# A two-layer streaming encoder on one core: weight units of the seven-product down projections made in five steps, and where those steps stand

## The chip, the cores and the metric

The kernel runs on one NeuronCore of a Trainium2 chip. The metric is device time in microseconds (us) of one execution; lower is better. Five engines work beside each other, each through its own queue in order: TensorE (PE, matmuls, with its weight loads shown apart as PEld), VectorE (DVE), ScalarE (ACT), GpSimd (POOL) and SyncE (SP, which here only issues DMA transfers). They meet through semaphores.

## The reference

One inference step of a two-layer hybrid encoder, for 512 prompt tokens and 32 sample tokens, which the kernel carries side by side as 544 columns. Each layer is a token mixer (an S5 state-space layer in layer 0, multi-scale retention in layer 1), memory cross-attention, and a causal ConvFFN, each with a residual. The change lies in the ConvFFN:

```python
def conv_ffn(h, conv_state, w_up, conv_w, conv_b, w_down):
    l = h.shape[1]
    u = h.astype(F32) @ w_up.astype(F32)
    a, g = jnp.split(u, 2, axis=-1)
    ext = jnp.concatenate([conv_state.astype(F32), a], axis=1)
    cw = conv_w.astype(F32)
    conv = cw[0] * ext[:, 0:l] + cw[1] * ext[:, 1:l + 1] + cw[2] * ext[:, 2:l + 2] + conv_b.astype(F32)
    y = (jax.nn.gelu(conv) * g) @ w_down.astype(F32)
    return y.astype(h.dtype), ext[:, l:]
```

Here `w_up` is 1024 x 5632 and `w_down` 2816 x 1024, all in float32.

## The kernel before

**Arithmetic.** Tokens lie along the free dimension, in two halves of 272 columns (`TH`). A float32 product is made of three matmuls on split operands: each operand is a rounded high part and a low part (the difference), and high x high, high x low and low x high are accumulated. `split` (L227) makes the two parts: a copy on ACT (L228), a subtraction on DVE (L229).

**Order.** The program is written with a tile framework (`TileContext(nc, schedule_with_timeline_sim=True)`, L1566): the text gives the operations and the buffers by tag and number, and a scheduler sets each engine's queue when the program is built. A buffer tag with `bufs=3` holds three tiles; a fourth waits until one is released.

**Up tiles.** `ffn_layer` (L1292) makes 22 feature tiles of 128 rows in three groups of 8, 8 and 6 (`FGROUPS`, L49). One pass of the loop (L1309) makes two dense tiles, one from `w_a` and one from `w_g` (`dense`, L272): each loads 512 KB of raw weights (tag `wr`, three buffers), splits them into `wh` and `wl` (three buffers each) and runs 8 x 6 = 48 matmuls. An epilogue on DVE, ACT and POOL (L1314 to L1328) makes the convolution, the gelu and the gate. After every second pass `tokens` (L1176) builds, out of two gated feature tiles, the seven right-hand operands of a 2 x 2 seven-product scheme, as high and low parts: b11, b21, b22 and the four sums t1 to t4.

**The down projection.** After each group `down` (L1196) multiplies the group's tiles with its part of `w_down`. Output tiles are taken in four pairs (`p` = 0 to 3); a pair takes seven products (`PRODUCTS`, L52) over `kps` = 4 or 3 pairs of input tiles, 3 x `kps` matmuls each, where the plain scheme would take eight. Each product is added into the residual `x` by DVE (`add`, L1226). A pair's products share two PSUM banks and a third for product 2 (`take`, L1241).

**Weight units.** The left-hand operands of a pair come as units (`unit_open`, L1139): a unit covers two input pairs (one for the odd rest; `unit_sizes`, L95), so that a pair has two units. A unit takes

- a load of the raw blocks into `wr` (SP, L1154),
- three sums into `ws`, one buffer: two on DVE (L1158, L1159), one on POOL (L1160),
- `hb`, the high part of the three plain blocks a11, a22, a12 (ACT, L1161), and `lb`, at first minus that (ACT, L1164); four buffers each,
- `wh`, the high part of the four sums (ACT, L1162), and `wl`, their low part (DVE, L1163); the same three buffers as the up tiles', except that every fourth unit (j % 4 == 1, L1146) has buffers of its own, `whx` and `wlx`,
- and `unit_close` (L1172): a transfer issued by POOL reads the plain blocks from memory again and adds them to `lb`, which makes it the low part.

Products 1, 2 and 4 use `hb` and `lb`, the others `wh` and `wl`.

**The order written out in `down`.** Pairs 0 and 1 are opened and closed first (L1249 to L1251), behind the last tokens in the text. Products 1 and 7 of both pairs and 2 of pair 0 are begun with all input pairs but the last (`early`) and finished with the last one (`late`), which needs the last tokens. For later pairs (L1266 on) a pair is closed just ahead of its product 1, and the next pair is opened as a whole behind product 3 of the pair before.

**Behind the layer.** `done` hands a finished output pair to `resid_done` (L320), which makes the next stage's operand parts `xh`, `xl` and the sum of squares. Retention's first two dense tiles go through `dense2` (L291): with `late=1` both tiles run over seven operands, with a hook that forms the norm's columns between them (`resid_r`, L378), and then over the last.

Of the kernel before, what the change touches and what calls it, by code (L numbers as in the profile page):

```python
# [9 lines left out]
F32 = mybir.dt.float32  # L10
F32R = mybir.dt.float32r
I32 = mybir.dt.int32
AF = mybir.ActivationFunctionType
# [4 lines left out]
P = 128  # L18
# [174 lines left out]
class Kernel:  # L193
# [942 lines left out]
            self.resid_done(m)  # L1136


    def unit_open(self, src, nk, j):  # L1139


        V, A, PL = self.nc.vector, self.nc.scalar, self.nc.gpsimd
        n = nk * P

        def buf(tag):
# [4 lines left out]
        raw = self.main.tile([P, 1024], F32, tag="wr", bufs=3, name=self.name("wr"))  # L1150
        hs, ls = buf("wh"), buf("wl")
        hb, lb = (self.fp.tile([P, 768], F32R, tag=t, bufs=4, name=self.name(t)) for t in ("hb", "lb"))
        sf = self.fp.tile([P, 1024], F32, tag="ws", bufs=1, name=self.name("ws"))[:, :4 * n]
        self.nc.sync.dma_start(out=raw[:, :4 * n], in_=src)  # L1154

        def two(a):
            return a.rearrange("p (b n) -> p b n", b=2)
        V.tensor_tensor(out=two(sf[:, :2 * n]), in0=two(raw[:, n:3 * n]), in1=raw[:, :n].unsqueeze(1).to_broadcast([P, 2, n]), op=OP.subtract)  # L1158
        V.tensor_tensor(out=sf[:, 2 * n:3 * n], in0=sf[:, n:2 * n], in1=raw[:, n:2 * n], op=OP.add)  # L1159
        PL.tensor_tensor(out=sf[:, 3 * n:], in0=raw[:, 3 * n:4 * n], in1=sf[:, 2 * n:3 * n], op=OP.subtract)  # L1160
        A.copy(hb[:, :3 * n], raw[:, n:4 * n])  # L1161
        A.copy(hs[:, :4 * n], sf)  # L1162
        V.tensor_tensor(out=ls[:, :4 * n], in0=sf, in1=hs[:, :4 * n].bitcast(F32), op=OP.subtract)  # L1163
        A.activation(out=lb[:, :3 * n], in_=hb[:, :3 * n].bitcast(F32), func=AF.Copy, scale=-1.0)  # L1164
        d = {}
        for q, name in enumerate(("a11", "a22", "a12")):
            d[name] = hb[:, q * n:(q + 1) * n], lb[:, q * n:(q + 1) * n]
        for q, name in enumerate(("s3", "s1", "s2", "s4")):
            d[name] = hs[:, q * n:(q + 1) * n], ls[:, q * n:(q + 1) * n]
        return d, lb[:, :3 * n], src[:, n:4 * n]  # L1170

    def unit_close(self, u):  # L1172

        self.nc.gpsimd.dma_start(out=u[1], in_=u[2], accum_op=OP.add)

    def tokens(self, g):  # L1176

        V, A = self.nc.vector, self.nc.scalar
        t = [self.fp.tile([P, T + 4], F32, tag="f", bufs=FB, name=self.name("f"))[:, :T] for _ in range(2)]
# [6 lines left out]
        d = {}  # L1186
        for src, names in ((g[1], ("b21", "b22")), (t[0], ("t1", "t2")), (t[1], ("t3", "t4"))):
            hi, lo = self.parts(src)
            for h, name in enumerate(names):
                d[name] = hi[:, h * TH:(h + 1) * TH], lo[:, h * TH:(h + 1) * TH]  # L1190
        both = self.slot(dt=F32R)
        d["b11"] = both[:, :TH], both[:, TH:]
        self.split(b11, *d["b11"])
        return d

    def down(self, src, ys, done):  # L1196

        kps = len(ys)
# [3 lines left out]
        units = {}  # L1202

        def begin(p):
# [43 lines left out]
        early, late = range(kps - 1), [kps - 1]  # L1248
        for p in range(2):  # L1249
            begin(p)  # L1250
            end(p)  # L1251
        take(0)
        take(1)
        for i in (1, 7):
            step(0, i, early)
        for i in (1, 7):
            step(1, i, early)
        step(0, 2, early)
        for i in (1, 7, 2):
            step(0, i, late)  # L1260
        step(0, 6)
        step(0, 4)
        for i in (1, 7):
            step(1, i, late)
        step(0, 5)
        for p in range(1, KT // 2):  # L1266
            if p > 1:
                end(p)
                take(p)
                step(p, 1)  # L1270
                step(p, 7)
            else:
                step(p, 2)
            step(p - 1, 3)
            done(2 * p - 2)
            done(2 * p - 1)
            if p + 1 < KT // 2 and p > 0:
                begin(p + 1)
            step(p, 6)
            if p > 1:  # L1280
                step(p, 2)
            step(p, 4)
            step(p, 5)
        step(KT // 2 - 1, 3)
        done(KT - 2)
        done(KT - 1)

    def ffn(self, l):
        with self.tc.tile_pool(name=f"ffn{l}", bufs=1) as self.fp:
# [2 lines left out]
    def ffn_layer(self, l):  # L1292
# [13 lines left out]
        self.resid_start(0 + 1 if l == 0 else None)  # L1306
        for n, size in enumerate(FGROUPS):
            ys, half = [], []
            for _ in range(size):  # L1309
                pa, pg = first if f == 0 else [self.dense(io[n_][l, f], xs) for n_ in ("w_a", "w_g")]  # L1310
                paf = pa.rearrange("p a b -> p (a b)")
                ext = slot(W + 2)

# [17 lines left out]
                    ys.append(self.tokens(half))  # L1331
                    half = []
                f += 1
            last = n == len(FGROUPS) - 1
# [256 lines left out]
```

## Time and profile before

| what | value |
|---|---|
| time, median of 3 runs | 1932.65 us (1930.83 to 1935.11) |
| profiled execution, its own time | 1933.26 us |
| its span in the trace | 1931.4 us |
| mean granted TensorE clock | 0.974 |
| matmuls of the down projections (L1224) | 1848 of 13551 |
| DMA, mean over the span | 105 GB/s |

The six down projections run from about 517 to 581, 668 to 730, 793 to 845, 1591 to 1655, 1742 to 1804 and 1867 to 1913 us. In a page of the profile, a group of instructions shows line, engine, operation, names of what it writes and reads, shape and count, then busy time and mean duration, then the engine's idle time just ahead of it and what ended that. A window row gives busy time and count of PE, PEld, DVE, ACT and POOL in a stretch, the granted clock, the busy share of the DMA engines and their rate.

### The profile page before, as it was taken

The page shows a single profiled execution, that of the slowest core. Times are in us where ns is not written, and L with a number is a line of the kernel's source. Part 1 is how long each engine was busy: PE and PEld are TensorE (multiplying, and loading weights), DVE is VectorE, ACT ScalarE, POOL GpSimd, SP SyncE. Part 2 cuts the span into 40 slices and gives each one's busy share as a digit, 9 for nine tenths or more (in the row PEclk, how much of TensorE's full clock was granted, in tenths as well). Part 3 has the DMA queues.
Part 4 walks back from the last instruction along what each step waited for, and adds up shares of the span by engine and source line. Part 5 has one row for each costly group of instructions (what it writes and reads, how often), then busy time and mean ns, then how long its engine had stood idle before and what let it go on. Part 6 is the DMA issues. An engine that isn't in the chain of part 4 may idle for free. (4 is left out here: it accounts for less than half of the span.)

```text
span 1931.4 us, 32994 instructions
## 1 busy us (share of the span) xinstructions
PE 1821.0 (94%) x13551; PEld 1716.0 (89%) x13551; DVE 1198.8 (62%) x2143; ACT 713.7 (37%) x1073; POOL 387.9 (20%) x512
## 2 busy tenths in 40 slices
PE   8878899999999989989999999999999998999996
PEld 7467799999989989879899898997899998998995
DVE  7988775547746646765555646448544665566573
ACT  3244554434424424523222222234433343353343
POOL 4655310022211312310000100001002221122122
PEclk9978999999999999989999999999999999999998
DMA  6647732123443433432222222223222244344232
GB/s 224 204 125 173 211 131 100 39 82 99 120 98 100 121 98 101 104 106 82 80 85 93 72 82 76 95 76 107 92 66 88 77 121 99 99 118 112 89 99 74
DMA packets 75191, 203.73 MB, mean 105 GB/s; under 512 B 9953, under 2 KB 20577, under 8 KB 75041
## 3 DMA queue, kind: packets, MB, share of 16 engines
q1 hardware_dynamic: 65536, 175.79, 28.0%
q0 software_dynamic: 9216, 25.69, 8.1%
q8 instruction: 106, 1.74, 0.4%
q14 instruction: 45, 0.36, 0.1%
q10 hardware_dynamic: 288, 0.15, 0.0%
HBM read 188.47 MB, written 10.77 MB: 103 GB/s over the span
## 5 line engine op out<-in xcount | busy, mean ns | idle before, releaser
L269 PE MATMUL ps<-xh,wh 128*128 128x272 f32 x2432 | 507.5, 289 | 7.8 <-DVE x L392 3.7
L269 PE MATMUL ps<-xh,wl 128*128 128x272 f32 x2432 | 504.7, 289 | 1.0 <-DVE wl L229 1.0
L269 PE MATMUL ps<-xl,wh 128*128 128x272 f32 x2432 | 503.5, 288 | 2.1 <-DVE xl L328 2.1
L228 ACT CAST wh<-wr 128x1024 fp32r<-128x1024 f32 x192 | 201.0, 1051 | 545.4 <-PE ps L269 428.0
L269 PEld LDWEIGHTS ps<-xh,wh 128*128 128x128 f32 x2432 | 383.4, 189 | 13.7 <-ACT r L334 3.9
L269 PEld LDWEIGHTS ps<-xh,wl 128*128 128x128 f32 x2432 | 382.0, 189 | 4.4 <-issue 2.3
L269 PEld LDWEIGHTS ps<-xl,wh 128*128 128x128 f32 x2432 | 382.6, 189 | 2.6 <-DVE xl L328 2.3
L229 DVE TENSOR_TENSOR wl<-wr,wh 128x1024 fp32r<-128x1024 f32 x192 | 240.9, 1258 | 93.9 <-ACT wh L228 89.5
L269 PE MATMUL ps<-r,wh 128*128 128x272 f32 x1280 | 214.5, 289 | 3.0 <-ACT r L976 1.6
L269 PEld LDWEIGHTS ps<-r,wh 128*128 128x128 f32 x1280 | 180.6, 188 | 6.4 <-ACT r L228 3.0
L1224 PE MATMUL ps<-r,wh 128*128 128x272 f32 x704 | 149.4, 307 | 17.0 <-ACT wh L1162 9.3
L1228 DVE TENSOR_TENSOR x<-ps,x 128x272 f32<-128x272 f32 x168 | 72.0, 439 | 129.4 <-PE ps L1224 128.4
L1224 PEld LDWEIGHTS ps<-r,wh 128*128 128x128 f32 x704 | 117.8, 201 | 24.3 <-DVE x L1228 13.3
L269 PE MATMUL ps<-r,wl 128*128 128x272 f32 x640 | 132.2, 288 | 0.0
L1224 PE MATMUL ps<-r,hb 128*128 128x272 f32 x528 | 106.6, 295 | 7.4 <-DVE r L229 5.3
L337 POOL TENSOR_TENSOR acc<-acc,r 128x544 f32<-128x544 f32 x36 | 57.2, 1588 | 251.3 <-ACT r L334 249.8
L1224 PE MATMUL ps<-r,wl 128*128 128x272 f32 x352 | 106.8, 304 | 0.8 <-DVE wl L1163 0.8
L269 PEld LDWEIGHTS ps<-r,wl 128*128 128x128 f32 x640 | 100.3, 188 | 0.0
L1224 PEld LDWEIGHTS ps<-r,hb 128*128 128x128 f32 x528 | 84.4, 191 | 11.0 <-DVE r L229 7.5
L1224 PE MATMUL ps<-r,lb 128*128 128x272 f32 x264 | 78.0, 299 | 14.9 <-DMA lb<-in_w_d 14.9
L1162 ACT CAST wh<-ws 128x1024 fp32r<-128x1024 f32 (+1 forms) x48 | 46.7, 973 | 107.2 <-POOL ws L1160 106.2
L392 DVE TENSOR_TENSOR x<-ps,x 128x544 f32<-128x544 f32 x48 | 34.5, 723 | 77.1 <-PE ps L269 77.1
(370 smaller groups left out, 2849.2 us busy)
## 6 DMA issues: line engine op xcount, KB each, us to landing
wr<-in_w_r SPq DMA_DIRECT2D x48, 512.0 KB, 3.7
wr<-in_w_a SPq DMA_DIRECT2D x44, 512.0 KB, 3.7
wr<-in_w_g SPq DMA_DIRECT2D x44, 512.0 KB, 3.7
wr<-in_w_d SPq DMA_DIRECT2D x40, 512.0 KB, 3.9
lb<-in_w_d POOLq DMA_DIRECT2D x40, 384.0 KB, 5.6
wr<-in_w_k SPq DMA_DIRECT2D x16, 512.0 KB, 4.7
wr<-in_w_v SPq DMA_DIRECT2D x16, 512.0 KB, 4.4
wr<-in_w_q SPq DMA_DIRECT2D x16, 512.0 KB, 4.1
```

The costliest lines, as they stand in the source:

```text
L228: self.nc.scalar.copy(hi, src)
L229: (self.nc.gpsimd if pool else self.nc.vector).tensor_tensor(out=lo, in0=src, in1=hi.bitcast(F32), op=OP.subtract)
L269: mm(ps[:, h, :TH], lhsT=ws[wi], rhs=x[xi][:, h * TH:(h + 1) * TH], start=start and n == 0, stop=stop and n == 2)
L337: add.tensor_tensor(out=self.acc, in0=self.acc, in1=sq, op=OP.add)
L392: self.nc.vector.tensor_tensor(out=self.halves(x), in0=src, in1=self.halves(x), op=OP.add)
L1162: A.copy(hs[:, :4 * n], sf)
L1224: mm(out, lhsT=w[wi], rhs=y[yi], start=start and k == 0 and m == 0, stop=stop and k == kps - 1 and m == 2, skip_group_check=not start)
L1228: self.nc.vector.tensor_tensor(out=x, in0=banks[p][i], in1=x, op=OP.add)
```

## The change

- `unit_open` and `unit_close` become `unit`, which returns five steps: `load` (SP), `sums` (the three sums, `hb`, `lb`), `first` (the cast `wh`), `close` (POOL's transfer) and `second` (the subtraction `wl`). In the text `lb` now stands ahead of `wh`.
- `down` returns three parts. `begin` (load both units of pair 0, make the first) stands ahead of the dense tiles of the group's last pass; `more` (close the first, make the second) stands between those dense tiles and their epilogue; `rest` (everything else) stands behind the last tokens, with product 2 of pair 1 now among the early ones.
- From pair 1 on, the next pair is loaded behind products 1 and 7, its first unit made behind product 6, closed and the second made behind product 4, and that one closed behind product 5.
- `tokens` makes b11 first, then b21 and b22, then the sums, then t3 and t4, then t1 and t2.
- Retention's first two tiles are called with `late=2`: six operands each, then the last two.

The number of instructions of each kind, the transfers and their sizes stay.

```diff
-    def unit_open(self, src, nk, j):
+    def unit(self, src, nk, j):
...
+        def load():
+            t["raw"] = self.main.tile([P, 1024], F32, tag="wr", bufs=3, name=self.name("wr"))
+            self.nc.sync.dma_start(out=t["raw"][:, :4 * n], in_=src)
+
+        def sums():
+            raw = t["raw"]
+            t["hs"], t["ls"] = buf("wh"), buf("wl")
...
+            V.tensor_tensor(out=two(sf[:, :2 * n]), in0=two(raw[:, n:3 * n]), in1=raw[:, :n].unsqueeze(1).to_broadcast([P, 2, n]), op=OP.subtract)
+            V.tensor_tensor(out=sf[:, 2 * n:3 * n], in0=sf[:, n:2 * n], in1=raw[:, n:2 * n], op=OP.add)
+            PL.tensor_tensor(out=sf[:, 3 * n:], in0=raw[:, 3 * n:4 * n], in1=sf[:, 2 * n:3 * n], op=OP.subtract)
+            A.copy(t["hb"][:, :3 * n], raw[:, n:4 * n])
+            A.activation(out=t["lb"][:, :3 * n], in_=t["hb"][:, :3 * n].bitcast(F32), func=AF.Copy, scale=-1.0)
...
+        def first():
+            A.copy(t["hs"][:, :4 * n], t["sf"])
+
+        def close():
+            self.nc.gpsimd.dma_start(out=t["lb"][:, :3 * n], in_=src[:, n:4 * n], accum_op=OP.add)
+
+        def second():
+            V.tensor_tensor(out=t["ls"][:, :4 * n], in0=t["sf"], in1=t["hs"][:, :4 * n].bitcast(F32), op=OP.subtract)
+
+        return d, load, sums, first, close, second
...
     def tokens(self, g):
...
+        both = self.slot(dt=F32R)
+        d["b11"] = both[:, :TH], both[:, TH:]
+        self.split(g[0][:, :TH], *d["b11"])
...
+        two(g[1], ("b21", "b22"))
...
-        for src, names in ((g[1], ("b21", "b22")), (t[0], ("t1", "t2")), (t[1], ("t3", "t4"))):
...
-        both = self.slot(dt=F32R)
-        d["b11"] = both[:, :TH], both[:, TH:]
-        self.split(b11, *d["b11"])
+        two(t[1], ("t3", "t4"))
+        two(t[0], ("t1", "t2"))
...
-    def down(self, src, ys, done):
+    def down(self, src, kps, done):
...
+        def load(p):
             for n, nk in enumerate(sizes):
                 c = 4 * P * first[n]
-                units[p, n] = self.unit_open(src[p][:, c:c + 4 * P * nk], nk, 2 * p + n)
-
-        def end(p):
-            for n in range(nu):
-                self.unit_close(units[p, n])
+                units[p, n] = self.unit(src[p][:, c:c + 4 * P * nk], nk, 2 * p + n)
+                units[p, n][1]()
+
+        def make(p, n):
+            for f in units[p, n][2:4]:
+                f()
+
+        def close(p, n):
+            for f in units[p, n][4:]:
+                f()
...
+        def begin():
+            load(0)
+            make(0, 0)
+
+        def more():
+            close(0, 0)
+            make(0, 1)
+
+        def rest(y):
+            ys.extend(y)
+            close(0, 1)
+            load(1)
+            make(1, 0)
+            early, late = range(kps - 1), [kps - 1]
+            take(0)
+            take(1)
+            step(0, 1, early)
+            step(0, 7, early)
+            step(0, 2, early)
+            close(1, 0)
+            make(1, 1)
+            close(1, 1)
+            step(1, 1, early)
+            step(1, 7, early)
+            step(1, 2, early)
+            for i in (1, 7, 2):
+                step(0, i, late)
+            step(0, 6)
+            step(0, 4)
+            step(1, 1, late)
+            step(1, 7, late)
+            step(0, 5)
+            step(1, 2, late)
+            for p in range(1, KT // 2):
+                go = p + 1 < KT // 2
+                if p > 1:
+                    take(p)
+                    step(p, 1)
+                    step(p, 7)
+                if go:
+                    load(p + 1)
+                step(p - 1, 3)
+                done(2 * p - 2)
+                done(2 * p - 1)
+                step(p, 6)
+                if go:
+                    make(p + 1, 0)
+                if p > 1:
+                    step(p, 2)
+                step(p, 4)
+                if go:
+                    close(p + 1, 0)
+                    make(p + 1, 1)
+                step(p, 5)
+                if go:
+                    close(p + 1, 1)
+            step(KT // 2 - 1, 3)
...
     def ffn_layer(self, l):
...
-            for _ in range(size):
+            last = n == len(FGROUPS) - 1
+            begin, more, rest = self.down(io[f"w_d{n}"][l], size // 2, (lambda m: self.resid_done(m, final=l == 1)) if last else (lambda m: None))
+            for i in range(size):
+                if i == size - 1:
+                    begin()
                 pa, pg = first if f == 0 else [self.dense(io[n_][l, f], xs) for n_ in ("w_a", "w_g")]
+                if i == size - 1:
+                    more()
...
-            self.down(io[f"w_d{n}"][l], ys, (lambda m: self.resid_done(m, final=l == 1)) if last else (lambda m: None))
+            rest(ys)
...
-        first = self.dense2([io["w_r"][n] for n in range(2)], xs, hooks=self.resid_r())
+        first = self.dense2([io["w_r"][n] for n in range(2)], xs, late=2, hooks=self.resid_r())
```

More of the change, by code (lines that the diff above doesn't have):

```diff
@@ L1136, in attention @@
             self.resid_done(m)
-    def unit_open(self, src, nk, j):
+    def unit(self, src, nk, j):
         V, A, PL = self.nc.vector, self.nc.scalar, self.nc.gpsimd
         n = nk * P
+        d, t = {}, {}
         def buf(tag):
@@ L1148, in buf @@
             return self.main.tile([P, 1024], F32R, tag=tag, bufs=3, name=self.name(tag))
[L1150 to L1174, printed above, removed]
+        def load():
+            t["raw"] = self.main.tile([P, 1024], F32, tag="wr", bufs=3, name=self.name("wr"))
+            self.nc.sync.dma_start(out=t["raw"][:, :4 * n], in_=src)
@@ new lines, in sums, with two @@
+        def sums():
+            raw = t["raw"]
+            t["hs"], t["ls"] = buf("wh"), buf("wl")
+            t["hb"], t["lb"] = (self.fp.tile([P, 768], F32R, tag=g, bufs=4, name=self.name(g)) for g in ("hb", "lb"))
+            sf = t["sf"] = self.fp.tile([P, 1024], F32, tag="ws", bufs=1, name=self.name("ws"))[:, :4 * n]
+            def two(a):
+                return a.rearrange("p (b n) -> p b n", b=2)
+            V.tensor_tensor(out=two(sf[:, :2 * n]), in0=two(raw[:, n:3 * n]), in1=raw[:, :n].unsqueeze(1).to_broadcast([P, 2, n]), op=OP.subtract)
[3 more added lines that the diff above has]
+            A.activation(out=t["lb"][:, :3 * n], in_=t["hb"][:, :3 * n].bitcast(F32), func=AF.Copy, scale=-1.0)
+            for q, name in enumerate(("a11", "a22", "a12")):
+                d[name] = t["hb"][:, q * n:(q + 1) * n], t["lb"][:, q * n:(q + 1) * n]
+            for q, name in enumerate(("s3", "s1", "s2", "s4")):
+                d[name] = t["hs"][:, q * n:(q + 1) * n], t["ls"][:, q * n:(q + 1) * n]
@@ L1176, in tokens @@
+        def first():
[5 more added lines that the diff above has]
+        return d, load, sums, first, close, second
     def tokens(self, g):
         V, A = self.nc.vector, self.nc.scalar
+        d = {}
+        both = self.slot(dt=F32R)
@@ L1179, in tokens, with two @@
+        d["b11"] = both[:, :TH], both[:, TH:]
+        self.split(g[0][:, :TH], *d["b11"])
+        def two(src, names):
+            hi, lo = self.parts(src)
+            for h, name in enumerate(names):
+                d[name] = hi[:, h * TH:(h + 1) * TH], lo[:, h * TH:(h + 1) * TH]
+        two(g[1], ("b21", "b22"))
         t = [self.fp.tile([P, T + 4], F32, tag="f", bufs=FB, name=self.name("f"))[:, :T] for _ in range(2)]
@@ L1185, in tokens @@
         V.tensor_tensor(out=t4, in0=b21, in1=t2, op=OP.subtract)
-        d = {}
-        for src, names in ((g[1], ("b21", "b22")), (t[0], ("t1", "t2")), (t[1], ("t3", "t4"))):
-            hi, lo = self.parts(src)
-            for h, name in enumerate(names):
-                d[name] = hi[:, h * TH:(h + 1) * TH], lo[:, h * TH:(h + 1) * TH]
-        both = self.slot(dt=F32R)
-        d["b11"] = both[:, :TH], both[:, TH:]
-        self.split(b11, *d["b11"])
-        return d
-    def down(self, src, ys, done):
-        kps = len(ys)
+        two(t[1], ("t3", "t4"))
+        two(t[0], ("t1", "t2"))
+        return d
+    def down(self, src, kps, done):
         sizes = unit_sizes(kps)
@@ L1201, in down @@
         nu = len(sizes)
-        units = {}
-        def begin(p):
+        units, ys = {}, []
+        def load(p):
             for n, nk in enumerate(sizes):
                 c = 4 * P * first[n]
-                units[p, n] = self.unit_open(src[p][:, c:c + 4 * P * nk], nk, 2 * p + n)
-        def end(p):
-            for n in range(nu):
-                self.unit_close(units[p, n])
+                units[p, n] = self.unit(src[p][:, c:c + 4 * P * nk], nk, 2 * p + n)
[6 more added lines that the diff above has]
+                f()
         banks = {}
@@ L1246, in take @@
             banks[p] = b
[L1248 to L1283, printed above, removed]
@@ L1284, in down @@
-        step(KT // 2 - 1, 3)
-        done(KT - 2)
-        done(KT - 1)
+        def begin():
[53 more added lines that the diff above has]
+            step(KT // 2 - 1, 3)
+            done(KT - 2)
+            done(KT - 1)
@@ L1288, in ffn @@
+        return begin, more, rest
     def ffn(self, l):
@@ L1333, in ffn_layer @@
                 f += 1
-            last = n == len(FGROUPS) - 1
-            self.down(io[f"w_d{n}"][l], ys, (lambda m: self.resid_done(m, final=l == 1)) if last else (lambda m: None))
+            rest(ys)
         nc.sync.dma_start(out=io["nconv"][l], in_=nco.rearrange("p f s c -> p (f s c)"))
```

## The prediction

> **What bounds the kernel now.** I read the page first: which engine is full, and what the projections' matmuls (line 1224) wait for.
>
> ```profile
> PE 1821.0 (94%) x13551; PEld 1716.0 (89%) x13551; DVE 1198.8 (62%) x2143; ACT 713.7 (37%) x1073; POOL 387.9 (20%) x512
> ...
> L1224 PE MATMUL ps<-r,wh 128*128 128x272 f32 x704 | 149.4, 307 | 17.0 <-ACT wh L1162 9.3
> ...
> L1224 PE MATMUL ps<-r,lb 128*128 128x272 f32 x264 | 78.0, 299 | 14.9 <-DMA lb<-in_w_d 14.9
> ```
>
> PE is the only engine near full, and the loops issue the same products after the change as before, so a gain can only come out of PE's waits. In the seven-product projections two kinds stand out: PE waits for a cast weight sum (`wh`, L1162), and 14.9 us for the landing of closing transfers (`lb`); call the latter **B**. The former sits in a cluster at the start of each projection, with other short waits. To size that cluster I count matmuls by stretch: first an undisturbed stretch of up tiles as yardstick, then each projection from its first matmul up to its first wait for `lb`, then the stretch of `lb` waits in the first one. Columns: stretch and length, busy time and count for PE, PEld, DVE, ACT and POOL, granted clock, DMA share, GB/s.
>
> ```profile
> 600.00:650.00 50.00, 50.00 (x402) 50.00 (x401) 33.71 (x56) 19.87 (x26) 12.02 (x22) 1.00 0.31 97
> ...
> 517.50:543.20 25.70, 22.98 (x162) 21.72 (x160) 14.46 (x29) 10.99 (x16) 6.69 (x9) 0.93 0.31 79
> 667.90:693.60 25.70, 22.89 (x162) 21.62 (x160) 14.56 (x29) 11.55 (x16) 7.50 (x10) 0.93 0.31 81
> 793.20:814.20 21.00, 18.64 (x132) 17.68 (x130) 12.83 (x29) 8.44 (x15) 4.73 (x7) 0.92 0.25 57
> 1590.50:1617.90 27.40, 24.59 (x162) 22.86 (x161) 15.39 (x31) 11.74 (x16) 7.25 (x10) 0.88 0.31 83
> 1741.50:1767.80 26.30, 24.17 (x162) 22.70 (x160) 14.24 (x28) 11.17 (x16) 7.32 (x10) 0.87 0.31 79
> 1866.50:1886.90 20.40, 18.57 (x132) 17.64 (x130) 12.97 (x30) 8.38 (x15) 4.82 (x7) 0.92 0.21 51
> ...
> 543.20:554.00 10.80, 7.38 (x54) 6.72 (x54) 6.04 (x10) 1.99 (x3) 1.58 (x2) 1.00 0.74 155
> ```
>
> Unhindered, a matmul of 272 columns takes 50.00 / 400 = 0.125 us (two of the 402 straddle the edges). The six first parts hold 4 x 162 + 2 x 132 = 912 matmuls, worth 114.0 us, and last 146.5 us in all: **A, 32.5 us lost at the start**. A and B together are 47.4 us, 2.5% of the span.
>
> **The change, part by part.** No instruction is added or dropped. Each unit keeps its load, three sums, three ACT operations, one DVE subtraction and one closing transfer, and the tokens keep theirs; they only change their place in the text. Does that matter? Only in part: each engine's work is placed at build time by when it is ready. The first unit's raw weights were cast at 493.55 (below), although that cast stands in the text behind the last up tile, which PE left only at 517.5. So text order counts where two things compete for a buffer or an engine, and those places are what I look for.
>
> *Start of a projection (A).* Below: that cast; the casts into `wh` in 490 to 530 (count, ns min/median/max, first and last start); the casts and subtractions of the last tokens; the last subtraction of a weight sum; PE's wait; the clock behind it.
>
> ```profile
> 493.55 0.83 ACT L1161 CAST hb<-wr 128x768 fp32r<-128x768 f32 x1 [1.50 <-DMA wr<-in_w_d]
> ...
> L1162 ACT CAST wh<-ws x4: 1029/1046/1048, 507.5 to 525.4; 128x1024 fp32r<-128x1024 f32 x4
> L228 ACT CAST wh<-wr x2: 1046/1046/1047, 494.3 to 502.4; 128x1024 fp32r<-128x1024 f32 x2
> ...
> L228 ACT CAST r<-f x4: 413/644/647, 521.6 to 526.9; 128x544 fp32r<-128x544 f32 x3, 128x272 fp32r<-128x272 f32 x1
> ...
> L229 DVE TENSOR_TENSOR r<-f,r x4: 433/717/718, 523.0 to 528.2; 128x544 fp32r<-128x544 f32 x3, 128x272 fp32r<-128x272 f32 x1
> ...
> 526.45 1.23 DVE L1163 TENSOR_TENSOR wl<-ws,wh 128x1024 fp32r<-128x1024 f32 x1 [1.70 <-ACT wh L1162]
> ...
> 526.47 0.52 PE L1224 MATMUL ps<-r,wh 128*128 128x272 f32 x2 [1.62 <-ACT wh L1162]
> ...
> 529.80:533.10 3.30, 3.30 (x14) 3.13 (x14) 2.07 (x6) 0.00 (x0) 0.73 (x1) 0.50 0.00 0
> ```
>
> The four units of the first two pairs pass through one buffer `ws`, so their casts come one behind the other, (525.4 - 507.5) / 3 = 6.0 us apart. The first waited for one of the three `wh` buffers: the two up-tile casts at 494.3 and 502.4 went ahead of it. The fourth ended at 526.4, and PE had stood 1.62 us. The last pass of the loop makes two up tiles (`w_a`, `w_g`), 48 matmuls or 6.0 us each, the second from 511.5 to 517.5. In the new text the first unit stands ahead of that pass's weights, so it takes the buffer that the 494.3 cast took. The two up-tile casts then get the buffers that fall free one up tile later, at 505.5 - 6.0 = 499.5 and at 505.5. Each still leads its first matmul by 6 us and needs 1.05 + 1.23. The second unit has buffers of its own (`whx`, `wlx`) and can follow by about 500. The third waits for a buffer until 511.5, the fourth until 517.5: cast to 518.6, subtracted to 519.9. PE asks for the fourth at its 43rd matmul, 517.5 + 42 x 0.125 = 522.8. The wait for L1162 goes, with 3 us to spare. On SP the two unit loads now go ahead of that pass's two; there are three raw buffers, each free once its split is done, so I see no wait there.
>
> What is late next is the tokens. The last subtraction ended at 528.2 + 0.43 = 528.7: 7.1 us from the first cast, for 4 subtractions of at most 0.72. It was b11's, whose source had been there since the tile before; the new text makes b11 first, then b21/b22, t3/t4, t1/t2, as the products ask. With the gate as late as now, t3/t4 come at 521.6 + 0.64 + 2 x 0.72 = 523.7, plus whatever of their DVE sums isn't covered; PE's 54 early matmuls end at 517.5 + 6.75 = 524.3. I leave 1.3 us a projection, 8 us in all, for unit work that gets in between.
>
> The last row shows a second cost: behind these waits PE ran at clock 0.50 for 3.3 us. By the clock column A holds 0.07 x 25.7 x 2 + 0.08 x 21.0 + 0.12 x 27.4 + 0.13 x 26.3 + 0.08 x 20.4 = 13.6 us of it; I take it to go with the waits. The Trainium skill ("TensorE: Matmul & The Clock Gate", section "Why this matters for your kernels") speaks against that: it asks for no idle gap above about 3 us between bursts, and the longest here is 1.62 us, so by the page the halving would have another cause and stay. The trace, so far, has it behind a cluster of short waits.
>
> Of A I take 32.5 - 8 = **-24.5 us**. Bounds: nothing, and all of it.
>
> *The closing transfers (B).* Pairs 2 and 3 of the first projection:
>
> ```profile
> 536.07 1.58 ACT L1161 CAST hb<-wr 128x768 fp32r<-128x768 f32 x2 [8.78 <-PE ps L1224]
> ...
> L1164 ACT ACTIVATE lb<-hb x4: 827/842/847, 537.6 to 542.4; 128x768 fp32r<-128x768 f32 x4
> L1174 POOL DMA_DIRECT2D lb<-in_w_d x4: 857/874/1017, 538.7 to 543.5; - x4
> ...
> DMA to landing us min/median/max: 5.0/8.4/9.1
> ```
>
> `hb` and `lb` have four buffers, two pairs' worth, so pair 2's cast waits for product 4 of pair 0 (8.78 us idle, ended by PE). All four closings of pairs 2 and 3 then left within 4.8 us and landed after 5.0 to 9.1 us. In the new text products 4 of pairs 0 and 1 stand 3 + 3 + 12 + 3 + 12 + 12 = 45 matmuls (5.6 us) apart, and each unit closes by itself. From the release to pair 2's first use lie 45 + 12 + 12 = 69 matmuls, 8.6 us. The chain needs two casts, 1.58, the copy, 0.84, POOL's issue, 0.87, and 5.0 us: 8.3; the second unit comes about 1 us later and is asked for 0.75 us later. That is even, so I keep 0.8 us a projection, and nothing in pair 3, which has 12 us. While POOL waits to issue a closing, the up tile's small POOL operations stand behind it, with an up tile of 6 us to catch up. B goes from 14.9 to 5, **-10 us**; bounds nothing and 15.
>
> *New waits.* Pair 2's sums need `wh` after product 3 of pair 0, which is 48 matmuls (6.0 us) ahead of product 7 of pair 2, and two units through one `ws` take 6.0 us and 1.23. I take 0.7 us a projection, **+4 us**; bounds 0 and 12 (2 us each, about PE's 1.62).
>
> *Retention's first two tiles (`late=2`).*
>
> ```profile
> 845.30:857.30 12.00, 7.63 (x36) 7.29 (x36) 8.96 (x19) 5.09 (x7) 1.44 (x2) 0.72 0.40 132
> ...
> 846.05 2.36 DVE L229 TENSOR_TENSOR wl<-wr,wh 128x1024 fp32r<-128x1024 f32 x2 [0.18 <-DMA decay<-in_decay]
> 848.33 2.59 DVE L328 SCALAR_TENSOR_TENSOR xl<-x,gains,xh 128x544 fp32r<-128x544 f32 x2
> ```
>
> 12.0 us for 36 matmuls, 7.5 lost. PE stood before operand 6 of tile 0, while tile 1's weights were ready at about 847.3, after the first of two subtractions. With operand 6 put off too, tile 1's six early operands, 36 matmuls or 4.5 us, fit into the wait for the last `xl`, at 850.9. **-4 us**; bounds 0 and 7.5.
>
> Sum: -24.5 - 10 + 4 - 4 = -34.5 us. The profiled execution took 1933.26 us, 1.9 beyond its span and 0.6 above the median of 1932.65, so it serves for both: 1933.3 - 34.5 = **1899 us**.
>
> **The rivals.**
> 1. *The closings stay late.* The DMA engines are 0.74 busy where `lb` is awaited, and a projection that starts sooner only meets the same transfer sooner. A, retention and the new waits alone: 1933.3 - 24.5 - 4 + 4 = 1909 us. Against it: a closing that left alone took 5.0 us.
> 2. *Nothing moves.* The steps already run when they are ready, as the 493.55 cast shows, and text order decides little: 1931 us. Against it: the first sum lost its buffer to two casts that the new text puts behind it.
> 3. *The clock stays halved*, by the gap rule above: three quarters of 13.6 us don't come back, 1899 + 10 = 1909 us. Against it: the place of the 0.50.
> 4. *Slower: the up tile starves.* If the third unit, too, gets its `wh` buffer ahead of the last up tile, that tile works with one. Its cast then starts when the tile before it ends; PE waits 1.05 + 1.23, some 2.4 us with the handoffs, twice, and the clock halves for 3.3 us (1.7 lost): 6.5 us in each of six projections, 39. ACT stands behind such casts, so I give A half (12) and B nothing: 1933.3 + 39 - 12 - 4 = 1956 us. It decides from the point where a tile's cast can't end before the tile ahead of it does: casts lead by 11 us now (494.3 for 505.5), by 6 with one buffer fewer, by nothing with two. Against it: the text puts the third unit behind the tile.
>
> **How the numbers follow.** Forecast 0.50; rival 1 0.20; rival 2 0.12; rival 3 0.08; rival 4 0.10. Measurements of this kernel can't tell less than about 0.2%, 3.9 us, from no change. Faster: 0.50 + 0.20 + 0.08 + 0.02 of rival 2 = 0.80; same 0.10; slower 0.10. Range: down to all of A, B and retention's 7.5 but for 1 us a projection, 32.5 + 14.9 + 7.5 - 6 = 49, 1884; up to half of A and nothing else, 1917, and 3 us towards rival 2, 1920.
>
> **What would show it.** A right: L1162 no longer heads PE's waits, the first parts shrink to about 22 us (18 in the small ones), clock 1.00 in them. B right: `lb` waits near 5 us, landings nearer 5 us. Retention right: PE busy between 847.3 and 851.8 of the old time. Wrong: PE waiting for L228 in the last up tiles (rival 4), or the four casts in their old order and place (rival 2).

## The result, and the profile after

The changed kernel takes 1914.78 us (median of 4 runs, 1913.13 to 1919.80) beside 1933.36 us of the kernel before (median of 4): ratio 0.9909, 95% interval 0.9888 to 0.9931. Faster by 0.9%, inside the range, and 16 us above the forecast of 1899. The profiled execution took 1914.82 us with a span of 1913.0, so 18.4 us of the span went.

In the changed kernel a product's matmul is line 1240 (it was 1224), the residual add 1244 (1228), the raw load 1153 (1154), the cast `wh` 1174 (1162), the closing transfer 1177 (1174) and the subtraction `wl` 1180 (1163). From the page after:

```profile
L1240 PE MATMUL ps<-r,wh 128*128 128x272 f32 x704 | 141.6, 298 | 15.2 <-DVE x L1244 10.0
...
L1240 PE MATMUL ps<-r,lb 128*128 128x272 f32 x264 | 77.1, 302 | 13.5 <-DMA lb<-in_w_d 13.5
```

The cast no longer heads PE's waits in the `wh` row: the residual adds do. The `lb` row, which was to fall to 5 us, went from 14.9 to 13.5. PE's waits of the whole execution, first before and then after (us in total, times, longest):

```profile
PE ps L1224 <- ACT wh L1162: 9.3, 7, 1.9
PE ps L1224 <- DVE x L1228: 8.2, 18, 0.7
PE ps L1224 <- DVE r L229: 5.3, 9, 1.5
```

```profile
PE ps L1240 <- DVE x L1244: 11.6, 20, 1.1
PE ps L1240 <- ACT wh L1174: 5.1, 7, 1.5
```

The waits for the tokens (`r`) are gone, those for the cast are halved, and those for the adds grew by 3.4 us. The first parts of the six projections after, each from its first matmul up to its first wait for `lb` (columns as in the prediction):

```profile
516.70:537.60 20.90, 19.30 (x150) 18.62 (x148) 15.77 (x30) 9.36 (x12) 5.51 (x9) 1.00 0.53 119
661.60:685.40 23.80, 22.23 (x162) 21.64 (x160) 17.46 (x33) 10.99 (x15) 5.50 (x9) 0.93 0.52 116
783.80:802.40 18.60, 17.33 (x132) 16.46 (x130) 13.08 (x28) 8.68 (x15) 5.11 (x7) 1.00 0.32 78
1579.40:1603.10 23.70, 22.05 (x162) 21.64 (x160) 17.39 (x33) 10.81 (x14) 5.59 (x9) 0.93 0.51 116
1726.00:1749.90 23.90, 22.20 (x162) 21.63 (x160) 17.59 (x33) 10.95 (x15) 5.64 (x9) 0.93 0.51 116
1847.90:1866.40 18.50, 17.25 (x132) 16.44 (x130) 13.17 (x29) 9.47 (x16) 5.26 (x8) 1.00 0.29 72
```

900 matmuls are worth 112.5 us at 0.125 us each, and the six parts last 129.4 us: A fell from 32.5 to 16.9 us, by 15.6. That is most of the 18.4 us. So the gain is at the start of the projections, where the prediction looked. Whether it has the prediction's cause is another matter, and the casts speak against that. From the timelines of ACT and of DVE after, the first, second and fourth cast, the cast of `hb` just ahead of the second, and the first subtraction (start, duration, the idle time before it and what ended it):

```profile
492.72 1.05 ACT L1174 CAST wh<-ws 128x1024 fp32r<-128x1024 f32 x1 [1.50 <-PE ps L269]
...
512.43 0.83 ACT L1166 CAST hb<-wr 128x768 fp32r<-128x768 f32 x1 [5.05 <-DMA wr<-in_w_d]
513.17 1.04 ACT L1174 CAST wh<-ws 128x1024 fp32r<-128x1024 f32 x1
...
525.48 1.05 ACT L1174 CAST wh<-ws 128x1024 fp32r<-128x1024 f32 x1 [2.23 <-POOL ws L1165]
```

```profile
506.35 1.27 DVE L229 TENSOR_TENSOR wl<-wr,wh 128x1024 fp32r<-128x1024 f32 x1
507.54 1.21 DVE L1180 TENSOR_TENSOR wl<-ws,wh 128x1024 fp32r<-128x1024 f32 x1
```

The first unit's cast took the place of the up tile's at 494.3, as forecast. Its subtraction came 15 us later, behind the up tile's own (L229), and until then the one buffer `ws` was held. So the second unit, forecast for about 500, was cast at 513.17, and the fourth at 525.48, where it had been before (525.4). The last 2 us of the second cast's delay have another cause: its sums were ready at 511.0 on GpSimd, but in ACT's order it stands behind the fourth unit's `hb`, and for that unit's raw data ACT waited 5.05 us.

If the last cast did not move, what gained? SP's queue did change. The first raw loads in its timeline before (start, length of the run of loads, count), what the first one waited for, and its timeline after:

```profile
489.86 23.50 SPq L1154 DMA_DIRECT2D wr<-in_w_d  x5
```

```profile
SPq L1154 <- DVE wl L229: 5.0, 1, 5.0
```

```profile
477.56 6.82 SPq L1153 DMA_DIRECT2D wr<-in_w_d  x2
485.34 0.33 SPq L233 DMA_DIRECT2D wr<-in_w_a  x1
489.02 0.33 SPq L233 DMA_DIRECT2D wr<-in_w_g  x1
```

Before, the first raw load stood 5.0 us on SP for a raw buffer that an up tile's subtraction freed, and left at 489.86. After, the two raw loads go first, from 477.56 on, and the last up tile's two behind them.

### The profile page after: what moved, and what is told of

Read it like the earlier page. It is cut to its first block, busy times and chain, and to the rows that moved or that the text cites. A ratio compares the mean times of both kernels' runs of the same rounds, so it can differ in the third digit from the quotient of the medians.

```text
span 1913.0 us, 33026 instructions
## 1 busy us (share of the span) xinstructions
PE 1811.5 (95%) x13551; PEld 1711.3 (89%) x13551; DVE 1196.2 (63%) x2143; ACT 715.0 (37%) x1073; POOL 393.1 (21%) x512
## 5 line engine op out<-in xcount | busy, mean ns | idle before, releaser
L269 PEld LDWEIGHTS ps<-xh,wh 128*128 128x128 f32 x2432 | 383.7, 189 | 13.7 <-ACT r L334 3.8
L228 ACT CAST wh<-wr 128x1024 fp32r<-128x1024 f32 x192 | 201.0, 1051 | 517.0 <-PE ps L269 398.5
L229 DVE TENSOR_TENSOR wl<-wr,wh 128x1024 fp32r<-128x1024 f32 x192 | 241.5, 1261 | 87.5 <-ACT wh L228 83.1
L269 PE MATMUL ps<-r,wh 128*128 128x272 f32 x1280 | 214.4, 289 | 3.0 <-ACT r L976 1.6
L269 PEld LDWEIGHTS ps<-r,wh 128*128 128x128 f32 x1280 | 180.8, 188 | 6.4 <-ACT r L228 3.0
L1240 PE MATMUL ps<-r,wh 128*128 128x272 f32 x704 | 141.6, 298 | 15.2 <-DVE x L1244 10.0
L1240 PEld LDWEIGHTS ps<-r,wh 128*128 128x128 f32 x704 | 112.8, 193 | 20.6 <-DVE x L1244 8.3
L1240 PE MATMUL ps<-r,lb 128*128 128x272 f32 x264 | 77.1, 302 | 13.5 <-DMA lb<-in_w_d 13.5
```

What stands on the lines that cost most here:

```text
L228: self.nc.scalar.copy(hi, src)
L229: (self.nc.gpsimd if pool else self.nc.vector).tensor_tensor(out=lo, in0=src, in1=hi.bitcast(F32), op=OP.subtract)
L269: mm(ps[:, h, :TH], lhsT=ws[wi], rhs=x[xi][:, h * TH:(h + 1) * TH], start=start and n == 0, stop=stop and n == 2)
L1240: mm(out, lhsT=w[wi], rhs=y[yi], start=start and k == 0 and m == 0, stop=stop and k == kps - 1 and m == 2, skip_group_check=not start)
```

## The experiments

Two theories stood after this. **Casts:** the early steps (sums, cast, transfer) carry the gain. **Tokens:** their new order does, since their waits went. The runs were to tell these apart, then the loop's steps and retention, and then why B stayed. Each ratio is to the kernel before on the same chip, with its 95% interval.

### Tokens alone

The kernel before with the new `tokens` and nothing else of the change:

```diff
...
+        self.split(g[0][:, :TH], *d["b11"])
+        two(g[1], ("b21", "b22"))
...
+        two(t[1], ("t3", "t4"))
+        two(t[0], ("t1", "t2"))
```

> The kernel before with one part of the change alone: the last tokens in the new order (b11, b21/b22, t3/t4, t1/t2); units and loop as before. Theory (the tokens carry the start's gain): the waits for DVE r and ACT r, 10.7 us before, 0.7 after, go, and the half-clock windows behind them shrink: 8 to 12 us off, ratio to before 0.994 to 0.996. Rival (the units' earlier steps carry it, the tokens only looked late because the units' work stood in their way): under 3 us off, ratio 0.998 to 1.000.

1936.27 us, ratio 0.9993 (0.9981 to 1.0005): nothing. PE's waits for `r` did fall, from 5.3 + 1.4 to 1.2 us, and its waits for the residual adds grew from 8.2 to 13.2 us.

### Everything but the early steps

```diff
-                if i == size - 1:
-                    begin()
...
-                if i == size - 1:
-                    more()
...
+            begin()
+            more()
             rest(ys)
```

> The changed kernel, but the first pair's steps stand behind the last up tile again, as before; tokens, loop and retention as changed. Theory (tokens carry the start, and the first pair's early steps give little, since the first unit's subtraction still waited behind both up tiles and the fourth cast stayed at 525.5): 1914 to 1918 us, ratio to before 0.990 to 0.992. Rival (the early steps carry it): 1923 us or more, ratio 0.995 or more.

1935.80 us, ratio 0.9998 (0.9984 to 1.0012). Without the early steps nothing is left of the gain. The tokens theory, on which both expectations leaned, falls.

### The loop's steps and retention as before

```diff
                 if p > 1:
+                    for n in range(nu):
+                        units[p, n][4]()
...
-                if go:
-                    load(p + 1)
...
                 if go:
-                    make(p + 1, 0)
+                    load(p + 1)
+                    for n in range(nu):
+                        make(p + 1, n)
+                        units[p + 1, n][5]()
```

> The changed kernel, but pairs 2 and 3 are made as before: load and all steps of both units behind the pair's residual adds, and both closings at the head of the next pair. Theory (the loop's steps moved no lb wait, 19.5 us lost before and 19.4 after): 1913 to 1918 us. Rival (the earlier steps did gain, and something else took it back): 1921 us or more, with lb waits of PE above 20 us.

1915.45 us, ratio 0.9894 (0.9879 to 0.9908). The loop's steps carry nothing of the gain, for a plain reason: in the traces of this kernel and of the changed one every engine runs the same instructions in the same order (13551 matmuls, 2143 on VectorE, 1073 on ScalarE, 512 on GpSimd, 482 transfers of SP). The scheduler put the steps where it had put them for the other text. For the chip the two are one program, and their times, 1914.78 and 1915.45 us, show how well a time repeats.

```diff
-        first = self.dense2([io["w_r"][n] for n in range(2)], xs, late=2, hooks=self.resid_r())
+        first = self.dense2([io["w_r"][n] for n in range(2)], xs, hooks=self.resid_r())
```

> The changed kernel with retention's first two tiles as before (late=1). Theory (the operands stand in the order set at build time, and PE's stalls of 2.44 and 2.09 us at 836 and 839 us are those of before): within 1 us of the changed kernel. Rival (the retention term of the prediction, 4 us, is in the 18 us gained): 1918 us or more.

1915.24 us, ratio 0.9894 (0.9878 to 0.9909). Retention carries nothing either. PE's waits there in the changed kernel (833 to 846 us):

```profile
PE ps L269 <- ACT xh L327: 2.3, 1, 2.3
PE ps L269 <- DVE xl L328: 1.8, 1, 1.8
```

The kernel before has the same two, 2.3 and 2.1 us: they stand as they stood.

### The raw loads alone, and with the tokens

What is left is the early steps, of which the raw loads are one. First the kernel without early steps (0.9998) with only its raw loads put back ahead of the last up tile:

```diff
+                if i == size - 1:
+                    load()
                 pa, pg = first if f == 0 else [self.dense(io[n_][l, f], xs) for n_ in ("w_a", "w_g")]
...
         def begin():
-            load(0)
             make(0, 0)
```

> The changed kernel, but of the first pair's steps only the raw loads stand ahead of the last up tile; its sums, casts, subtractions and closings stand behind that tile, as in the run with the old start (1930 us). Theory (what counts is that VectorE doesn't stand for the raw load, 12.9 us in all): VectorE's wait for wr falls from 12.7 to about 1 us and the time to 1916 to 1922 us. Rival (the casts' place counts, VectorE's 27 us of waits for wh with tokens behind them): the wait for wr falls, but the time stays at 1927 us or more.

1917.64 us, ratio 0.9901 (0.9881 to 0.9920): the loads bring the whole gain back. Then the changed kernel with the old order of the tokens:

```diff
...
-        two(g[1], ("b21", "b22"))
...
+        for src, names in ((g[1], ("b21", "b22")), (t[0], ("t1", "t2")), (t[1], ("t3", "t4"))):
...
-        two(t[1], ("t3", "t4"))
-        two(t[0], ("t1", "t2"))
```

> The changed kernel with the tokens in the order of before (b21/b22, t1/t2, t3/t4, b11). Since neither the tokens' order alone nor everything but the first pair's early steps gained anything, two theories are left. Early steps alone (VectorE no longer stands 12.9 us for the raw loads and 26.4 us, now 15.7, for the casts, with the tokens queued behind): 1914 to 1919 us. Both together (each without the other is worth nothing): 1927 us or more.

1921.40 us, ratio 0.9922 (0.9907 to 0.9937): between the two theories, some 6 us above the changed kernel's 1915.24 of the run beside it with `late=1`. So the tokens' order is worth something once the loads are early. Two runs on the kernel before settle it, the loads alone and the loads with the tokens' order:

```diff
             for i in range(size):
+                if i == size - 1:
+                    raws = []
+                    for nk in unit_sizes(size // 2):
+                        raws.append(self.raw(src[0][:, c:c + 4 * P * nk], nk))
+                        c += 4 * P * nk
                 pa, pg = first if f == 0 else [self.dense(io[n_][l, f], xs) for n_ in ("w_a", "w_g")]
```

Here `raw` makes a unit's raw tile and its load, and the unit that is opened later takes that tile.

> The kernel before with one thing alone: the first pair's two raw loads stand ahead of the last up tile's; tokens, steps, loop and retention as before. Theory (the raw loads are what carried the gain: the first was issued at 489.9 when an up tile's buffer came free, and goes at about 478 now; the tokens' order is worth 6 us on top, as the run with the old tokens showed): 1918 to 1924 us, ratio to before 0.991 to 0.994. Rival (the loads help only with the new order of the tokens): 1930 us or more, ratio above 0.997.

1925.93 us, ratio 0.9957 (0.9942 to 0.9971).

> The kernel before with two things alone: the first pair's two raw loads ahead of the last up tile's (alone 0.9957 of the time before) and the last tokens in the new order (alone 0.9993). Theory (these two are the whole of the gain, the tokens' order being worth something only once the casts come earlier): 1914 to 1919 us, ratio 0.989 to 0.992. Rival (the two only add up, and the steps in the loop carry the rest): 1923 us or more, ratio 0.994 or more.

1916.84 us, ratio 0.9910 (0.9889 to 0.9931): two edits of the change give what all of it gives, within the intervals. They don't add up: the loads alone are worth 0.43%, the tokens alone nothing, and both 0.90%.

The traces show the same at the place of the gain. For each kernel the six first parts are counted here up to the start of the same matmul (the 163rd, in the third groups the 133rd); the loss to the clock is worked out from the clock column, as for A. All in us, from the profiled executions:

| kernel | six first parts | of it lost to the clock |
|---|---|---|
| before | 153.2 | 13.7 |
| tokens alone | 151.5 | 12.1 |
| loads alone | 146.3 | 8.5 |
| loads and tokens | 136.6 | 3.5 |
| changed | 140.5 | 5.3 |

What stands in the way there can be seen in the first projection. Its first part with the tokens alone, with the loads alone and with both:

```profile
518.50:544.60 26.10, 23.83 (x162) 22.73 (x160) 14.54 (x29) 10.82 (x15) 6.12 (x9) 0.87 0.32 81
```

```profile
517.00:542.20 25.20, 23.33 (x162) 21.87 (x160) 14.16 (x28) 9.37 (x14) 6.88 (x8) 0.93 0.32 81
```

```profile
518.50:541.20 22.70, 21.07 (x161) 20.15 (x160) 13.76 (x27) 8.76 (x13) 6.26 (x8) 1.00 0.35 91
```

The same 162 matmuls (161 in the last, one having fallen over the edge) take 26.1, 25.2 and 22.7 us. PE's longest waits in these parts, in the same order (all of them in the last):

```profile
PE ps L1228 <- ACT wh L1162: 1.1, 1, 1.1
PE ps L1228 <- DVE x L1232: 0.8, 1, 0.8
```

```profile
PE ps L1229 <- ACT wh L1167: 0.7, 1, 0.7
PE ps L1229 <- DVE r L229: 0.5, 1, 0.5
```

```profile
PE ps L1233 <- DVE x L1237: 1.1, 1, 1.1
PE ps L1233 <- DVE wl L1168: 0.3, 1, 0.3
PE ps L1233 <- DVE r L229: 0.2, 1, 0.2
```

Each edit alone takes one link out of a chain of short waits and leaves another: the cast's wait without the loads, the cast's and the tokens' without the new order. With both, the wait for the cast is gone from this part, and its clock is 1.00 (0.87 and 0.93 with one edit); two of the other five parts still show 0.93. That this chain carries the whole gain is read from the traces and was not tested apart. How an earlier load brings the casts forward can be read off ACT. The tokens alone, then the loads and the tokens; PE enters the products at 518.5 in both:

```profile
505.86 0.83 ACT L1161 CAST hb<-wr 128x768 fp32r<-128x768 f32 x1 [1.46 <-DMA wr<-in_w_d]
...
509.68 1.03 ACT L1162 CAST wh<-ws 128x1024 fp32r<-128x1024 f32 x1
...
526.21 1.04 ACT L1162 CAST wh<-ws 128x1024 fp32r<-128x1024 f32 x1 [2.52 <-POOL ws L1160]
```

```profile
506.41 1.05 ACT L1167 CAST wh<-ws 128x1024 fp32r<-128x1024 f32 x1 [0.91 <-PE ps L269]
...
524.78 1.05 ACT L1167 CAST wh<-ws 128x1024 fp32r<-128x1024 f32 x1 [2.52 <-POOL ws L1165]
```

With the loads early, the first cast starts in the moment that PE lets its buffer go, 506.41. With the loads late, ACT stands 1.46 us for the third unit's raw data, and the first unit's cast, behind this in ACT's order, starts 3.3 us later. 1.4 us of this reach the fourth cast. The first expectation of this group took VectorE's waits for raw data for the measure. In its run they went, as expected, and with the loads and the tokens they are 0.9 us. But with the loads alone they are 12.8 us, as before (12.9), and 0.43% is gained all the same, so they are not the whole measure.

### The subtraction first

The step that kept `ws`, moved behind its cast:

```diff
         def make(p, n):
-            for f in units[p, n][2:4]:
+            for f in units[p, n][2:4] + units[p, n][5:]:
...
         def close(p, n):
-            for f in units[p, n][4:]:
+            for f in units[p, n][4:5]:
```

> The changed kernel with one step moved: each unit's subtraction stands right behind its cast, so that the one buffer ws is free before the last up tile's own steps; the closings keep their place. Theory (ws, held until that subtraction at 508.8 us, kept the four casts late): the second unit's sums follow the first's by about 6 us, the fourth cast starts near 519 instead of 525.5, PE's waits for wh (15.2 us on the line of the products) fall to under 6, and the time to 1904 to 1909 us. Rival 1 (the next wait takes it, DVE being crowded by the tokens): within 2 us of 1914.8. Rival 2 (the subtraction of 1.2 us ahead of the up tile's own starves that tile): 1918 us or more, with PE waiting for the up tiles' wl.

1908.46 us, ratio 0.9858 (0.9840 to 0.9875). Time and casts came as in the theory. The tiles `ws` of 488 to 525 us, and PE's waits of the whole execution:

```profile
L1174 ACT CAST wh<-ws x4: 1047/1051/1053, 493.3 to 517.3; 128x1024 fp32r<-128x1024 f32 x4
L1180 DVE TENSOR_TENSOR wl<-ws,wh x4: 1210/1214/1226, 495.2 to 519.2; 128x1024 fp32r<-128x1024 f32 x4
```

```profile
PE ps L1240 <- DMA lb<-in_w_d: 14.7, 17, 1.7
PE ps L1240 <- DVE x L1244: 9.7, 20, 0.7
...
PE ps L1240 <- ACT wh L1174: 2.2, 2, 1.8
```

The fourth cast comes at 517.3 and its subtraction ends at 519.2 + 1.2 = 520.4: the prediction had 517.5 and 519.9. The waits for the cast fall from 5.1 to 2.2 us. (The 15.2 us of the expectation are all the idle time of that row, the residual adds' 10.0 among it; the row still has 12.5.) Only the second unit's sums came later than expected, 14 us behind the first's. The chain now runs as the prediction had written it for the change, and the six first parts, counted as in the table above, take 126.4 us with the clock at 1.00 in all of them.

### The closing transfers

In the run above B still stands at 14.7 us. The closings were split, the third that product 1 needs going first:

```diff
-            self.nc.gpsimd.dma_start(out=t["lb"][:, :3 * n], in_=src[:, n:4 * n], accum_op=OP.add)
+            for a, b in ((0, n), (n, 3 * n)):
+                self.nc.gpsimd.dma_start(out=t["lb"][:, a:b], in_=src[:, n + a:n + b], accum_op=OP.add)
```

> The kernel with the subtraction first (1908.5 us), and each closing transfer in two: the third that product 1 needs (128 KB, a11), then the other two thirds. Theory (the landing is set by the bytes that the DMA engines still have ahead of it; the four closings of two pairs take them about 10 us): the first parts land in 3 to 4 us, PE's waits for lb fall from 14.7 to under 8 us, and the time to 1900 to 1904 us. Rival 1 (each transfer takes its 5 us whatever its size): lb waits stay near 15 us and the time within 2 us of 1908.5. Rival 2 (GpSimd's issue, 0.87 us a transfer, becomes the bound): lb waits above 16 us, slower than 1910.

1907.54 us, ratio 0.9857 (0.9841 to 0.9872). PE's waits of the whole execution:

```profile
PE ps L1241 <- DVE x L1245: 14.3, 27, 1.7
...
PE ps L1241 <- DMA lb<-in_w_d: 3.7, 8, 0.8
```

The `lb` waits fell by 11.0 us, as the theory had it, and the time stayed. The landings were not the theory's: the 48 transfers of 128 KB, 40 of them such first parts, landed 5.2 us after their issue in the median, not 3 to 4. Of the 11.0 us, 4.6 came back as waits for the residual adds (9.7 to 14.3) and 1.8 as waits for the up tiles' subtractions (1.0 to 2.8); where the rest went isn't shown. The profiled execution took 1910.33 us, 2.8 above its median, and in it the third groups last 95.1 us in place of 92.9; in a second execution of either program (the next two runs) it is 92.6 in place of 93.2, so the third groups did not get longer. Why the adds are late was to be tried: in the third groups VectorE also works on the finished residual rows, so that work was put behind the next pair's unit steps in the text.

```diff
                 step(p - 1, 3)
-                done(2 * p - 2)
-                done(2 * p - 1)
+                if not go:
+                    done(2 * p - 2)
+                    done(2 * p - 1)
...
                 if go:
                     close(p + 1, 1)
+                    done(2 * p - 2)
+                    done(2 * p - 1)
```

> The kernel with the subtraction first (1908.5 us), with one more step moved: in each pair but the last, the work on the finished residual rows stands behind the next pair's unit steps instead of ahead of them. Only the third group of each layer has such work, 10 to 13 us lost in each, with VectorE's sums for the next pair behind subtractions of 1.9 us. Theory (PE's waits for wh and wl there come of that queue): the two third groups lose 4 to 5 us less each, the time falls to 1899 to 1903 us. Rival (the work on the rows comes late at the end of the layer instead, where the next stage's first tile waits for it): 1907 us or more, with longer waits for xl behind the third groups.

1908.56 us, ratio 0.9866 (0.9847 to 0.9885): nothing. But the edit did not reach the queues. Every engine runs the same instructions in the same order as with the subtraction first alone, and the work on the rows (`xl`, L328) stands where it stood, behind the same subtraction of a weight sum. VectorE in the third group, with the subtraction first and then in this run:

```profile
800.10 1.22 DVE L1180 TENSOR_TENSOR wl<-ws,wh 128x1024 fp32r<-128x1024 f32 x1
801.24 1.89 DVE L328 SCALAR_TENSOR_TENSOR xl<-x,gains,xh 128x544 fp32r<-128x544 f32 x1
```

```profile
800.95 1.22 DVE L1180 TENSOR_TENSOR wl<-ws,wh 128x1024 fp32r<-128x1024 f32 x1
802.09 1.89 DVE L328 SCALAR_TENSOR_TENSOR xl<-x,gains,xh 128x544 fp32r<-128x544 f32 x1
```

With the closings split as well (by PE's waits above, splitting took away 11.0 us and gave back 4.6 in waits for adds, not 12 and 11):

> The kernel with the subtraction first and the split closings (1907.5 us), with the residual rows' work moved as in the run beside it. Splitting alone took 12 us of waits for lb away and gave back 11 in waits for VectorE's residual adds, most of them in the third groups. Theory (those adds were late behind the same queue on VectorE): 1896 to 1901 us, 2 to 4 us below the run beside it. Rival (the adds wait for something else, the subtractions of the weight sums among them): within 2 us of the run beside it.

1906.84 us, ratio 0.9856 (0.9837 to 0.9875): no more than the run beside it, and again the same instructions in the same order. So neither run tests the queue of the residual rows, and what holds the third groups stays open. What the two give is a second execution of each program: the `lb` waits are 17.3 and 3.6 us in it, those for the adds 10.2 and 12.6. The four runs with the subtraction first lie within 1.8 us of each other, 1.3 to 1.4% below the kernel before, and the plainer program, with that one step moved, is the one to keep.

## Why the prediction was right, and where it was wrong

Direction and place were right: the gain is in the waits at the start of the projections, and none of it in a place that the prediction left out. The size was off, and so was the cause. The time lies near the upper end of the range, which was worked out as half of A and nothing else; that it lies inside is luck in part, since what carried the gain is a move that the sum has at nothing.

- **A: -24.5 forecast, -15.6 measured.** The step that failed is "the second unit has buffers of its own and can follow by about 500". It counted buffers `wh` and forgot that the subtraction, which frees `ws`, stands in `second`, called by `more` behind the last up tile's weights. With the subtraction moved, the chain ran as written (fourth cast 517.3) and 6 us more went. By the count of the table the six first parts are then 26.8 us shorter than before (153.2 to 126.4), about what was forecast for A.
- **A's cause.** "On SP the two unit loads now go ahead of that pass's two [...] I see no wait there" was said of the kernel after, and the wait was in the kernel before: 5.0 us for a raw buffer, in the row of SP's queue. The prediction gave the loads no price. With the tokens' order they are the whole gain (0.9910 beside 0.9909). That the tokens are "what is late next" was right in a sharper sense than meant: alone they are worth nothing, on top of the loads 9 us (1925.93 to 1916.84).
- **The clock.** 13.6 us of halved clock in A became 0.07 x (23.8 + 23.7 + 23.9) = 5.0 us. Rival 3 had it stay; it went with the waits, as far as they went. The Trainium skill ("TensorE: Matmul & The Clock Gate", section "Why this matters for your kernels") asks for no idle gap above about 3 us. The traces disagree: in the first projection the clock was lost behind waits of 1.1 us and less, with one edit (0.87, 0.93), and not with both (1.00).
- **B: -10 forecast, -1.4 measured.** For this term rival 1 came true. The step "each unit closes by itself" changed nothing, since the queues are the same with the loop's steps written as before. (Two executions of one program, with the subtraction first, differ by more than these 1.4 us, 14.7 and 17.3.) The cover was mis-sized: the first row below is the stretch from the release of `hb` (pair 2's first cast, 530.05) to PE's first wait, 62 matmuls or 7.55 us and not 69 or 8.6, since product 5 of pair 1 came behind product 1 of pair 2. And of the landings only the shortest came near 5 us. The other rows are the closings in 528 to 552 us: the first left at 532.7, 2.65 us after the release, much as forecast (1.58 + 0.84), and they landed after 5.2 to 8.2 us.

```profile
530.05:537.60 7.55, 7.55 (x62) 7.50 (x60) 3.18 (x7) 4.79 (x6) 2.01 (x3) 1.00 0.69 138
```

```profile
L1177 POOL DMA_DIRECT2D lb<-in_w_d x4: 861/966/1229, 532.7 to 540.8; - x4
...
DMA to landing us min/median/max: 5.2/6.3/8.2
```

- **New waits: +4 forecast, +3.4 measured**, but on the residual adds (8.2 to 11.6 us) and not on a `wh` buffer: the number was met by luck.
- **Retention: -4 forecast, 0 measured.** The step "with operand 6 put off too, tile 1's six early operands fit into the wait" failed: the two waits kept their length, and `late=1` gives the same time.
- **Rivals 2 and 4.** The steps ahead of the last up tile do move with the text (the first cast went from 507.5 to 492.7); those in the loop do not, as rival 2 had it. No up tile starved: PE's waits for the up tiles' casts (L228 `wh`) are 1.8 us in both kernels.

Together: 15.6 of A, and 41.8 - 39.4 = 2.4 us in the rest of the projections (before, 349.7 us for 2203 matmuls of 0.125 us, 74.3 lost; after, 331.7 us, 56.3 lost), make 18.0 of the 18.4 us, by windows from each projection's first matmul to its last. In the rest, less waiting for `lb` and for the clock pays for more waiting for adds.

## What to carry to other kernels

Before pricing a moved step, look up what its load waits for on the queue in the kernel before: a load that stands for a shared buffer can be the whole gain, though it computes nothing. A buffer is held until its last reader has run, so a step split into parts must keep that reader near. And where short waits follow each other at one place, one removed alone may show nothing: try them together before dropping any. Where a scheduler sets the queues, compare the queues of the two kernels before reading a time: three of the twelve edits here changed the text and no queue.

## What was not expected of the hardware

The clock's loss is not decided by the waits alone. In the profiled execution of the changed kernel the first and the second projection have the same two waits at the same place (PE's waits of 524.0 to 527.5 and of 669.0 to 672.5 read alike):

```profile
PE ps L1240 <- DVE x L1244: 1.0, 1, 1.0
PE ps L1240 <- ACT wh L1174: 0.6, 1, 0.6
```

Behind them the clock differs:

```profile
527.00:530.00 3.00, 2.96 (x24) 2.75 (x23) 2.81 (x6) 0.00 (x0) 0.46 (x1) 1.00 0.42 145
672.00:675.00 3.00, 3.00 (x16) 3.00 (x15) 1.83 (x4) 0.00 (x0) 0.00 (x0) 0.52 0.40 138
```

24 matmuls in the first stretch, 16 in the second. Nor does the program decide: in the run with the loop's steps as before, which is the same program, the first projection has the same two waits of 1.0 and 0.6 us, and behind them

```profile
528.40:531.40 3.00, 3.00 (x14) 3.00 (x14) 1.61 (x2) 0.00 (x0) 0.00 (x0) 0.50 0.44 160
```

So the clock of one projection in one execution says little, and the sums over six say more. What tells the cases apart, no run shows; a forecast of such a loss needs a range that holds both.
